# Second norm's scale and shift by TensorE, roots by ScalarE and VectorE, one row by DMA, in a pooling block with a convolutional MLP

## The chip, the cores and the metric

The kernel runs on one core of a Trainium2 chip. Times are microseconds (us) on the device. A core has five engines that run their own instructions in order and wait for each other on semaphores: TensorE (PE, matrix products; PEld is its weight load), VectorE (DVE), ScalarE (ACT), GpSimd (POOL) and SyncE (SP), whose queue issues all of the DMA transfers here.

## What is computed

One layer (DEPTH is 1, so the mixer is the pooling one and the context tokens have no part in the output) on 1024 tokens of width 1024, in float32:

```python
def rms_norm(x, g):
    x32 = x.astype(jnp.float32)
    y = x32 * lax.rsqrt(jnp.mean(x32 * x32, axis=-1, keepdims=True) + EPS)
    return (y * g.astype(jnp.float32)).astype(x.dtype)
...
sh1, sc1, g1, sh2, sc2, g2 = ada_mods(c, ada_w[i], ada_b[i])   # silu(c) @ w + b, six rows of 1024
u = modulate(rms_norm(x, mix_pre_g[i]), sh1, sc1)              # u * (1 + sc1) + sh1
y = pool_mixer(u, pool_w[j], pool_scale[j])                    # four window means, minus u, times four 256x256 matrices
x = x + g1 * rms_norm(y, mix_post_g[i])
f = conv_ffn(modulate(rms_norm(x, ffn_pre_g[i]), sh2, sc2),    # up to 2 x 2816, 3-tap convolution over tokens,
             ffn_w_up[i], ffn_conv_w[i], ffn_conv_b[i], ffn_w_down[i])   # gelu(gate) * val, down to 1024
x = x + g2 * rms_norm(f, ffn_post_g[i])
```

There are four norms over the width: of x, of the mixer's output y, of the sum (the MLP's input), and of the MLP's output. Their mean squares and roots are called x, y, z and o in the kernel.

## The kernel before

Tokens stand on the 128 partitions in eight tiles `x.0` to `x.7`. The program lists its operations with their reads, writes and an estimated time each; a list scheduler at the top of the file then gives them an order for each engine by the longest estimated tail behind an operation, under the room that is left (50 pages of 128x1024 floats, 8 PSUM banks). What it produces is a fixed order for each engine; on the chip each engine goes through its own list and waits where it must. So a changed estimate or a changed operation moves others.

The work runs in these stages.

- **Pooling.** The window means are matrix products with a band matrix that carries the row's root (`band.j`, products `dq`, copies `dt`). For the root, ScalarE squares a tile and sums it along the row (`squares`, into `ms...`), GpSimd adds EPS and raises to the power -0.5 (`rstd`, two instructions, three where the square came in two parts plus one more), and VectorE scales the band.
- **Rows of the condition.** Each of the six rows is silu(c) times a 1024x1024 matrix, loaded in eight pages. `macs` does it on VectorE, one multiply-add pass over 128x1024 for each page, and TensorE sums over the partitions (`cs`, for a row laid out in columns; `g1q`, for a row spread over all partitions). `strips` does it on TensorE: two products of 32 x 512 for each page into one PSUM bank (`st`), a copy by ScalarE (`.acc`) and column sums (`cs`). The MLP's scale and shift come in two halves of 512 columns each, `a2.0.h` (scale) and `a2.1.h` (shift); before, `TUNE["strips"]` names only those of h = 0, and those of h = 1 are sixteen VectorE passes over 128x512.
- **Mixer.** Products `yq.j` with the four matrices, two banks for each token tile, in the order 1, 3, 4, 2, 5, 6, 0, 7. Tiles 0 and 7 need the shift row `sh1` (a VectorE `macs` row) at their edges (`de`). Then, for a tile: squares of yq (two parts), root `ry`, `ty` = yq times the row `grb` (gain times gate), `x` = x + ty * ry, squares of x, root `rz`, `xn` = x * rz. `grb` is a gain row `gr` that TensorE spreads over the partitions (`bcast`, products `rb`) and ScalarE copies, times `g1q`.
- **MLP input.** `xn` of four tiles is transposed (`tq`, first half of the tokens from tiles 1 to 4, second half from 5, 6, 7, 0), scaled and shifted into `u`, and split into a high and a low part (`B11`, `B21` for the first half of the tokens and columns 0 to 511 and 512 to 1023, `B12`, `B22` for the second half), because every product of the MLP is three matrix products of parts (lines L713 to L715).
- **MLP.** Four column blocks (0, 22, 1, 23) are computed plainly in four quarters: `hq`, 64 groups of three products. The other forty go through seven block products in place of eight for two blocks at a time (`X`, `Y`, `Z`), with sums `Bt1` to `Bt4` of the B parts. Then the convolution, gelu, gate, and the down projection in the same manner (`xq`, `zq`, `yb`), with the last norm tile by tile.

Of the kernel before, what the change touches and what calls it, by code (L numbers as in the profile page):

```python
# [195 lines left out]
def pool_ffn_block(ctx, tc, x, c_cols, ada, ada2, ada_bc, ada_br, gains_c, gains_r, pool_w,  # L196
# [359 lines left out]
    macs("g1", NK, first=False)
    for h in range(2):
        op(pe(0.86), lambda e, h=h: e.matmul(t(f"g1q.{h}"), ones, lo_("g1", h), start=True, stop=True), f"g1:{h}",
           f"g1q.{h}")
# [547 lines left out]
```

## Time and profile before

| | |
|---|---|
| three runs | 755.21, 755.69, 756.21 us (median 755.69) |
| profiled execution | 755.83 us, of it 754.1 us span of the engines' instructions |
| TensorE | busy 725.9 us, 96% of the span; mean granted clock 0.979 of full speed |
| VectorE, ScalarE, GpSimd | busy 606.3, 373.7 and 53.0 us |
| from DRAM and to DRAM | 101.91 MB and 19.92 MB |

The profiled execution is 0.14 us above the median. The span is the time from the first instruction to the last; some 1.7 us lie around it. A timeline row gives the start, the duration and, in brackets, how long the engine had stood idle and what released it. TensorE rows count a float32 product as two records, one pass of the weights each.

### The profile page before, as it was taken

The page shows a single profiled execution, that of the slowest core. Times are in us where ns is not written, and L with a number is a line of the kernel's source. Part 1 is how long each engine was busy: PE and PEld are TensorE (multiplying, and loading weights), DVE is VectorE, ACT ScalarE, POOL GpSimd, SP SyncE. Part 2 cuts the span into 40 slices and gives each one's busy share as a digit, 9 for nine tenths or more (in the row PEclk, how much of TensorE's full clock was granted, in tenths as well). Part 3 has the DMA queues.
Part 4 walks back from the last instruction along what each step waited for, and adds up shares of the span by engine and source line. Part 5 has one row for each costly group of instructions (what it writes and reads, how often), then busy time and mean ns, then how long its engine had stood idle before and what let it go on. Part 6 is the DMA issues. An engine that isn't in the chain of part 4 may idle for free.

```text
span 754.1 us, 8995 instructions
## 1 busy us (share of the span) xinstructions
PE 725.9 (96%) x3295; PEld 599.1 (79%) x3295; DVE 606.3 (80%) x759; ACT 373.7 (50%) x546; POOL 53.0 (7%) x73
## 2 busy tenths in 40 slices
PE   7996798999999999999999999999999999999996
PEld 6865686788888888888888888888888888887885
DVE  3986977999877777777777777776879886999974
ACT  6645336865444444444444444444634434337630
POOL 5044014000000000000000000000000000000051
PEclk9997979999999999999999999999999999999998
DMA  8998711013322222222222222206596267998852
GB/s 344 403 399 330 278 56 56 1 56 111 110 83 80 80 80 80 80 79 84 84 83 84 85 84 84 84 28 191 200 356 215 71 193 260 337 380 272 303 194 112
DMA packets 47285, 122.44 MB, mean 162 GB/s; under 512 B 5764, under 2 KB 5892, under 8 KB 47240
## 3 DMA queue, kind: packets, MB, share of 16 engines
q1 hardware_dynamic: 47240, 121.86, 44.9%
q8 instruction: 26, 0.43, 0.2%
q14 instruction: 19, 0.16, 0.1%
HBM read 101.91 MB, written 19.92 MB: 162 GB/s over the span
## 4 chain that ended last, share of the span: by engine, by line
PE 88%; DVE 5%; POOL 2%; DMA 2%; issue 1%; ACT 1%; SPq 0%; DVEq 0%; POOLq 0%; ACTq 0%
PE X L714 10%; PE X L713 10%; PE X L715 10%; PE xq L713 5%; PE xq L715 5%; PE xq L714 5%; PE Z L714 5%; PE Z L715 5%; PE Z L713 5%; PE dq L481 3%; PE zq L713 3%; PE zq L714 3%; PE zq L715 3%; PE Y L714 2%; PE Y L715 2%; PE Y L713 2%
## 5 line engine op out<-in xcount | busy, mean ns | idle before, releaser
L781 ACT ACTIVATE cv<-h,cv 128x1024 f32<-128x1024 f32 x44 | 54.8, 1246 | 104.0 <-DVE h L753 103.2
L783 DVE SCALAR_TENSOR_TENSOR cv<-h,cv,cv 128x1023 f32<-128x1023 f32 x44 | 56.5, 1283 | 24.1 <-ACT cv L781 24.0
L785 DVE SCALAR_TENSOR_TENSOR cv<-h,cv,cv 128x1023 f32<-128x1023 f32 x44 | 56.3, 1279 | 0.8
L747 ACT COPY h<-X 128x512 f32<-128x512 f32 (+1 forms) x80 | 35.8, 474 | 16.4 <-PE X L715 16.4
L753 DVE TENSOR_TENSOR h<-Z,h 128x384 f32<-128x384 f32 (+1 forms) x40 | 15.1, 418 | 33.2 <-PE Z L715 33.2
L879 DVE TENSOR_TENSOR dn<-dn,dn 128x512 f32<-128x512 f32 x55 | 37.2, 685 | 0.0
L970 POOL MEMSET g<- 128x1024 f32 x1 | 1.0, 952 | 496.8 <-PE xq L715 496.8
L753 DVE TENSOR_TENSOR h<-X,h 128x384 f32<-128x384 f32 (+1 forms) x40 | 15.1, 418 | 17.3 <-PE X L715 17.3
L761 DVE TENSOR_TENSOR cv<-cv,cv 128x1024 f32<-128x1024 f32 x22 | 26.8, 1217 | 0.2
L789 ACT ACTIVATE cv<-cv 128x1024 f32<-128x1024 f32 x22 | 23.4, 1063 | 7.0 <-DVE cv L785 4.9
L604 PE MATMUL yq<-wa,dt 128*128 128x256 f32 x96 | 26.4, 435 | 0.0
L604 PEld LDWEIGHTS yq<-wa,dt 128*128 128x128 f32 x96 | 20.9, 222 | 6.0 <-DVE grb L562 0.8
L747 ACT COPY h<-Z 128x384 f32<-128x384 f32 (+1 forms) x40 | 12.9, 376 | 23.7 <-PE Z L715 23.7
L367 ACT ACTIVATE xn<-yq 128x512 f32<-128x512 f32 x16 | 9.5, 597 | 24.0 <-PE yq L604 24.0
L481 PE MATMUL dq<-band,x 128*128 128x136 f32 (+2 forms) x160 | 20.8, 291 | 0.0
L402 DVE SCALAR_TENSOR_TENSOR g<-g,sc,g 128x1024 f32<-128x1024 f32 x14 | 17.9, 1282 | 3.3 <-DMA g<-in_ada 3.2
L481 PEld LDWEIGHTS dq<-band,x 128*128 128x128 f32 x160 | 20.5, 203 | 0.0
L1005 ACT ACTIVATE jk<-ca 128x512 f32<-128x512 f32 (+1 forms) x9 | 5.2, 579 | 23.5 <-DVE ca L1041 23.5
L879 DVE TENSOR_TENSOR dn<-du,dn 128x512 f32<-128x512 f32 x22 | 15.0, 684 | 0.0
L378 POOL TENSOR_SCALAR rso<-mso 128x1 f32<-128x1 f32 x8 | 7.1, 890 | 105.7 <-ACT jk L1005 105.2
L830 DVE TENSOR_TENSOR s<-s,w 128x512 f32<-128x512 f32 x20 | 13.8, 691 | 0.7
L833 DVE TENSOR_TENSOR s<-w,w 128x512 f32<-128x512 f32 x20 | 13.7, 685 | 0.0
(2803 smaller groups left out, 2379.8 us busy)
## 6 DMA issues: line engine op xcount, KB each, us to landing
w<-in_w_up SPq DMA_DIRECT2D x44, 512.0 KB, 5.1
dn<-gd SPq DMA_DIRECT2D x66, 256.0 KB, 4.9
dn<-in_w_down SPq DMA_DIRECT2D x66, 256.0 KB, 5.3
gd<-cv SPq DMA_DIRECT2D x22, 512.0 KB, 3.0
g<-in_ada SPq DMA_DIRECT2D x16, 512.0 KB, 6.7
a<-in_ada SPq DMA_DIRECT2D x16, 512.0 KB, 10.3
du<-in_w_down SPq DMA_DIRECT2D x22, 256.0 KB, 4.3
x<-in_x SPq DMA_DIRECT2D x8, 512.0 KB, 6.0
```

Source lines behind the costliest of these rows:

```text
L481: e.matmul(t(f"dq.{h}.{g}.{cx}")[:, lo - h * H:hi - h * H], t(f"x.{j}")[:, ch:ch + P], bview(j)[:, g, lo - o:hi - o], start=first, stop=la ...
L604: e.matmul(t(f"yq.{j}.{b}")[:, (g % 2) * 256:(g % 2 + 1) * 256], lt, rt, start=(k == 0 and g % 2 == 0), stop=(k == 1), skip_group_check=True)
L713: e.matmul(o, ah[:, s], bh, start=first, stop=False, skip_group_check=True)
L714: e.matmul(o, ah[:, s], bl, start=False, stop=False, skip_group_check=True)
L715: e.matmul(o, al[:, s], bh, start=False, stop=last, skip_group_check=True)
L747: e.copy(t(o)[:, lo:hi], t(b)[:, q:q + hi - lo])
L753: e.tensor_tensor(t(o)[:, lo:hi], t(b)[:, q:q + hi - lo], t(o)[:, lo:hi], ADD)
L761: op(engs or dve(1024), lambda e: e.tensor_tensor(t(o), t(a), t(b), al), f"{a} {b}", o, after=after)
L781: op(act(1024), lambda e: e.activation(t(o), t(h), AF.Identity, bias=cv[:, f, 3:4], scale=cv[:, f, 1:2]), f"{h} cv", o)
L783: op(("V", 1.2), lambda e: e.scalar_tensor_tensor(t(o)[:, 1:T], t(h)[:, 0:T - 1], cv[:, f, 0:1], t(o)[:, 1:T], MUL, ADD), f"{h} cv", o)
L785: op(("V", 1.2), lambda e: e.scalar_tensor_tensor(t(o)[:, 0:T - 1], t(h)[:, 1:T], cv[:, f, 2:3], t(o)[:, 0:T - 1], MUL, ADD), f"{h} cv", o)
L879: op(dve(H), lambda e: e.tensor_tensor(lo_(o, oh), lo_(a, ah), lo_(b, bh), al), f"{a}:{ah} {b}:{bh}", f"{o}:{oh}", after=after)
```

## The change

1. **Roots.** `rstd` leaves GpSimd. ScalarE adds the parts of a mean square (Identity with the other part as bias, once where there are two parts, twice for three) and takes the root (Sqrt with EPS as bias); VectorE takes the reciprocal. This holds for all 32 roots. A first small Sqrt right after the Tanh at the start loads the function table there.
2. **Strips.** `TUNE["strips"]` also names `a2.0.1` and `a2.1.1`, so all four halves of the MLP's scale and shift go through TensorE. The estimate of a pair of strip products falls from 1.1 to 0.45 us. (The code for strips of `sc1` and `g1`, with a table `selb`, is added as well, but the list doesn't name them: those rows and `sh1` stay on VectorE.)
3. **Gain row.** `grb` is loaded by one DMA that reads the row 128 times; the two `rb` products and the two ScalarE copies for it are gone.

```diff
-    "strips": ("a2.0.0", "a2.1.0"),
+    "strips": ("a2.0.0", "a2.1.0", "a2.0.1", "a2.1.1"),
...
+    A.activation(cst("root", [P, 1]), eps, AF.Sqrt)
...
+            elif n == "gr":
+                pg("grb")
+                small_load(lambda: t("grb"), gains_r[1:2].partition_broadcast(P), "grb", 1.4)
...
         def fn(e):
-            ms = stat["m" + key]
-            for k in range(2, n):
-                e.tensor_tensor(ms[:, 1:2], ms[:, 1:2], ms[:, k:k + 1], ADD)
-            e.tensor_scalar(r, ms[:, 0:1], EPS, ms[:, 1:2] if n > 1 else 0.0, ADD, ADD)
-            e.tensor_tensor(r, r, mhalf, ALU.pow)
-        op(("P", 0.7 + 0.2 * n), fn, "", f"m{key} r{key}")
+            for k in range(1, n):
+                e.activation(ms[:, 0:1], ms[:, 0:1], AF.Identity, bias=ms[:, k:k + 1])
+            e.activation(r, ms[:, 0:1], AF.Sqrt, bias=eps)
+        op(("A", 0.25 * n), fn, "", f"m{key} q{key}")
+        op(("V", 0.2), lambda e: e.reciprocal(r, r), f"q{key}", f"r{key}")
...
-            op(pe(1.1), fn, page, b)
+            op(pe(0.45), fn, page, b)
...
-    S.cls = "gr"
-    bcast("gr", 1, "gr", "grb")
```

With other operations and estimates the scheduler gives another order up to the middle of the MLP's first blocks. Three places show it.

On ScalarE, where the roots of tiles 4 and 2 are taken (msz and rsz are mean square and root of the MLP's input, a2_0_0_acc and a2_1_0_acc the copies of the strips for scale and shift of columns 0 to 511), before:

```order
L367 ACTIVATE xn_4_539,msz4_142<-x_4_256 128x1024
L658 CAST pl_22_h__630<-w_22_587 128x1024
L240 ACTIVATE xn_4_539<-x_4_256,rsz4_143 128x1024
L437 COPY a2_0_0_acc_651<-st_a2_0_0_560 128x512
L367 ACTIVATE xn_2_600,msz2_146<-x_2_223 128x1024
L437 COPY a2_1_0_acc_661<-st_a2_1_0_566 128x512
L367 ACTIVATE xn_5_672,msy5_148<-yq_5_0_646 128x512
```
and now:

```order
L454 COPY a2_0_0_acc_583<-st_a2_0_0_561 128x512
L375 ACTIVATE xn_2_596,msy2_152<-yq_2_0_576 128x512
L375 ACTIVATE xn_2_596,msy2_152<-yq_2_1_591 128x512
L386 ACTIVATE msy2_152<-msy2_152 128x1
L387 ACTIVATE rsy2_153<-msy2_152,eps_75 128x1
L375 ACTIVATE xn_1_487,msz1_142<-x_1_216 128x1024
L387 ACTIVATE rsz1_143<-msz1_142,eps_75 128x1
L375 ACTIVATE xn_3_512,msz3_146<-x_3_239 128x1024
L387 ACTIVATE rsz3_147<-msz3_146,eps_75 128x1
L454 COPY a2_1_0_acc_641<-st_a2_1_0_604 128x512
L375 ACTIVATE xn_4_540,msz4_150<-x_4_264 128x1024
L375 ACTIVATE xn_2_596,msz2_154<-x_2_231 128x1024
```
The copies of the strips stood behind the scaling of tile 4, which needs GpSimd's root rsz4. Now the scale's copy stands ahead of all work on tile 2, the shift's copy ahead of the squares of tile 4, and the scaling of tile 4 has gone to VectorE.

On VectorE, around the multiply-add passes of the row sh1 (a2_0_1_acc and a2_1_1_acc are the passes of the MLP's scale and shift for columns 512 to 1023), before:

```order
L402 SCALAR_TENSOR_TENSOR sh1_acc_735<-sh1_2_777,sc_78,sh1_acc_735 128x1024
L644 SCALAR_TENSOR_TENSOR a2_0_1_acc_658<-a2_0_1_2_613,sc_78,a2_0_1_acc_658 128x512 x2
L644 SCALAR_TENSOR_TENSOR a2_1_1_acc_674<-a2_1_1_2_655,sc_78,a2_1_1_acc_674 128x512 x2
L402 SCALAR_TENSOR_TENSOR sh1_acc_735<-sh1_3_803,sc_78,sh1_acc_735 128x1024
L402 SCALAR_TENSOR_TENSOR sh1_acc_735<-sh1_4_813,sc_78,sh1_acc_735 128x1024
L402 SCALAR_TENSOR_TENSOR sh1_acc_735<-sh1_5_824,sc_78,sh1_acc_735 128x1024
L402 SCALAR_TENSOR_TENSOR sh1_acc_735<-sh1_6_833,sc_78,sh1_acc_735 128x1024
L402 SCALAR_TENSOR_TENSOR sh1_acc_735<-sh1_7_844,sc_78,sh1_acc_735 128x1024
L644 SCALAR_TENSOR_TENSOR a2_0_1_acc_658<-a2_0_1_3_623,sc_78,a2_0_1_acc_658 128x512 x2
L644 SCALAR_TENSOR_TENSOR a2_1_1_acc_674<-a2_1_1_3_663,sc_78,a2_1_1_acc_674 128x512 x2
L659 TENSOR_TENSOR pl_23_l__881<-w_23_695,pl_23_h__716 128x1024
```
and now:

```order
L640 SCALAR_TENSOR_TENSOR x_5_270<-ty_5_768,rsy5_157,x_5_270 128x1024
L411 SCALAR_TENSOR_TENSOR sh1_acc_786<-sh1_1_800,sc_79,sh1_acc_786 128x1024
L674 TENSOR_TENSOR a2_1_86<-cs_a2_0_1_818,abc_69 128x4
L676 SCALAR_TENSOR_TENSOR a2_1_86<-a2_1_86,gc_70 128x4
L411 SCALAR_TENSOR_TENSOR sh1_acc_786<-sh1_2_812,sc_79,sh1_acc_786 128x1024
L674 TENSOR_TENSOR sh2_1_88<-cs_a2_1_1_826,abc_69 128x4
L411 SCALAR_TENSOR_TENSOR sh1_acc_786<-sh1_3_824,sc_79,sh1_acc_786 128x1024
L411 SCALAR_TENSOR_TENSOR sh1_acc_786<-sh1_4_835,sc_79,sh1_acc_786 128x1024
L732 TENSOR_TENSOR B21_0_l__873<-u_2_0_846,B21_0_h__861 128x512
L411 SCALAR_TENSOR_TENSOR sh1_acc_786<-sh1_5_849,sc_79,sh1_acc_786 128x1024
L411 SCALAR_TENSOR_TENSOR sh1_acc_786<-sh1_6_864,sc_79,sh1_acc_786 128x1024
L250 TENSOR_SCALAR u_3_0_879<-u_3_0_879,a2_1_86,sh2_1_88 128x512
```
The eight passes of a2 that stood among those of sh1 are gone (eight more stood further up). In their place stand the work of tile 5 and the splits of the B21 parts, which came later before.

On TensorE, from the end of the mixer's tile 6 to the next MLP quarter (cs_sh1 is the column sum of sh1, B21 the second quarter's input), before:

```order
L604 MATMUL yq_6_0_839<-wa_0_447,dt_1_0_372 128x256 x2
L604 MATMUL yq_6_0_839<-wa_0_447,dt_1_1_384 128x256 x2
L416 MATMUL cs_sh1_859<-ones_74,sh1_acc_735 128x1 x8
L416 MATMUL cs_a2_0_1_876<-ones_74,a2_0_1_acc_658 128x1 x4
L416 MATMUL cs_a2_1_1_886<-ones_74,a2_1_1_acc_674 128x1 x4
L713 MATMUL hq_23_0_896<-B11_0_h__728,pl_23_h__716 128x512
```
and now:

```order
L739 MATMUL hq_23_0_857<-B11_1_l__754,pl_23_h__773 128x512
L740 MATMUL hq_23_0_857<-B11_1_h__740,pl_23_l__795 128x512
L629 MATMUL yq_6_0_902<-wa_0_444,dt_1_0_374 128x256 x2
L629 MATMUL yq_6_0_902<-wa_0_444,dt_1_1_395 128x256 x2
L629 MATMUL yq_6_1_916<-wa_1_450,dt_1_2_418 128x256 x2
L629 MATMUL yq_6_1_916<-wa_1_450,dt_1_3_466 128x256 x2
L425 MATMUL cs_sh1_932<-ones_74,sh1_acc_786 128x1 x8
L738 MATMUL hq_0_0_748<-B21_0_h__861,pl_0_h__676 128x512
L739 MATMUL hq_0_0_748<-B21_0_l__873,pl_0_h__676 128x512
```
Before, the MLP's block 23 and half of tile 6 still stood behind the column sum of sh1, with the two column sums of a2 between. Now all four blocks of the first quarter, tile 6 and the column sums of a2 stand ahead of it, and the second quarter follows at once.

## Rows read from the trace of the kernel before

**Rows 1.** The page of the profile: busy time by engine, granted clock in 40 slices, chain.

```profile
PE 725.9 (96%) x3295; PEld 599.1 (79%) x3295; DVE 606.3 (80%) x759; ACT 373.7 (50%) x546; POOL 53.0 (7%) x73
...
PEclk9997979999999999999999999999999999999998
...
PE 88%; DVE 5%; POOL 2%; DMA 2%; issue 1%; ACT 1%; SPq 0%; DVEq 0%; POOLq 0%; ACTq 0%
```

**Rows 2.** Windows, six stages: length, busy time of each engine, clock, DMA share, GB/s.

```profile
28.40:57.90 29.50, 29.50 (x138) 19.84 (x138) 26.60 (x37) 14.43 (x34) 9.71 (x10) 0.94 1.02 402
57.90:90.80 32.90, 21.38 (x101) 18.26 (x100) 26.95 (x34) 15.59 (x27) 7.11 (x9) 0.84 0.84 320
90.80:105.30 14.50, 13.76 (x51) 12.34 (x52) 11.25 (x24) 3.03 (x6) 0.00 (x0) 0.54 0.06 25
105.30:126.40 21.10, 18.00 (x83) 14.99 (x81) 15.38 (x20) 12.16 (x24) 11.78 (x14) 1.00 0.25 101
126.40:154.40 28.00, 27.19 (x131) 21.85 (x132) 27.18 (x30) 23.84 (x35) 0.00 (x0) 1.00 0.04 11
154.40:747.00 592.60, 592.46 (x2641) 490.95 (x2639) 481.32 (x582) 285.02 (x388) 13.48 (x15) 1.00 0.42 146
```

**Rows 3.** Timeline of TensorE: start, duration, what, count, [idle before, what ended it].

```profile
65.42 3.57 PE L446 MATMUL cs_a<-sel,a_acc 128*128 128x1 f32 x16 [7.52 <-ACT a_acc L437]
...
91.28 3.54 PE L416 MATMUL cs_sh<-ones,sh_acc 128*128 128x1 f32 x16 [3.63 <-DVE sh_acc L402]
...
105.76 0.39 PE L713 MATMUL hq<-B_h__912,pl_h__590 128*128 128x512 f32 x1
...
126.39 1.75 PE L682 MATMUL tq<-ident,xn 128*128 128x128 f32 x14 [3.10 <-DVE xn L242]
...
154.06 0.39 PE L713 MATMUL X<-B_h__728,g_h__855 128*128 128x512 f32 x1
```

**Rows 4.** Timeline of ScalarE where a copy stands behind a wait, same columns.

```profile
63.75 1.15 ACT L240 ACTIVATE xn<-x,rsz 128x1024 f32<-128x1024 f32 x1 [5.22 <-POOL rsz L379]
64.81 0.57 ACT L437 COPY a_acc<-st_a 128x512 f32<-128x512 f32 x1
```

**Rows 5.** A group of GpSimd: busy us, mean ns of one, idle before and its releaser.

```profile
L379 POOL TENSOR_TENSOR rsz<-rsz,mhalf 128x1 f32<-128x1 f32 x8 | 10.4, 1300 | 0.7
```

**Rows 6.** Groups of VectorE from 28 to 154 us, same columns.

```profile
L613 DVE TENSOR_TENSOR ty<-yq,grb 128x512 f32<-128x512 f32 x16 | 10.6, 685 | 3.8 <-ACT xn L367 3.6
L644 DVE SCALAR_TENSOR_TENSOR a_acc<-a,sc,a_acc 128x512 f32<-128x512 f32 x14 | 10.2, 749 | 0.3
L615 DVE SCALAR_TENSOR_TENSOR x<-ty,rsy,x 128x1024 f32<-128x1024 f32 x8 | 10.1, 1279 | 0.8 <-POOL rsy L379 0.8
...
L402 DVE SCALAR_TENSOR_TENSOR sh_acc<-sh,sc,sh_acc 128x1024 f32<-128x1024 f32 x7 | 9.0, 1283 | 0.2
L761 DVE TENSOR_TENSOR u<-u,u 128x1024 f32<-128x1024 f32 x6 | 7.3, 1221 | 0.1
```

**Rows 7.** Timelines of ScalarE and VectorE: small operations and the function-table load.

```profile
2.42 0.21 ACT L303 ACTIVATE th<-cc 128x8 f32<-128x8 f32 x1 [0.41 <-DMA cc<-in_c_cols]
4.96 1.06 ACT L367 ACTIVATE band<-x 128x1024 f32<-128x1024 f32 x1 [2.33 <-DMA x<-in_x]
...
156.24 1.28 ACT L789 ACT_TABLE_LOAD   x1
157.54 1.06 ACT L789 ACTIVATE cv<-cv 128x1024 f32<-128x1024 f32 x1
...
2.86 0.17 DVE L305 TENSOR_TENSOR sc<-th,cc 128x8 f32<-128x8 f32 x1
```

**Rows 8.** A group of TensorE from 28 to 154 us: the strips.

```profile
L434 PE MATMUL st_a<-a,scx 128*32 128x512 f32 x32 | 4.7, 598 | 0.0
```

**Rows 9.** Timeline of the end, GpSimd and VectorE.

```profile
747.94 0.43 POOL L377 TENSOR_TENSOR mso<-mso 128x1 f32<-128x1 f32 x1 [5.97 <-ACT jk L1005]
...
749.45 1.42 DVE L1015 SCALAR_TENSOR_TENSOR ca<-ca,rso,x 128x512 f32<-128x512 f32 x2 [1.13 <-POOL rso L379]
```

More of the change, by code (lines that the diff above doesn't have):

```diff
@@ L287, in pool_ffn_block @@
     ident, ones = cst("ident", [P, P]), cst("ones", [P, P])
-    mhalf, scx, sel = cst("mhalf", [P, 1]), cst("scx", [P, NK, 32]), cst("sel", [P, 3])
+    eps, scx, sel = cst("eps", [P, 1]), cst("scx", [P, NK, 32]), cst("sel", [P, 3])
+    selb = cst("selb", [P, 2, P])
     sc, th = cst("sc", [P, NK]), cst("th", [P, NK])
@@ L295, in pool_ffn_block @@
     nc.sync.dma_start(out=cc, in_=c_cols)
-    V.memset(mhalf, -0.5)
+    V.memset(eps, EPS)
+    PL.memset(selb, 0.0)
     V.memset(ones, 1.0)
@@ L301, in pool_ffn_block @@
         V.memset(sel[32 * q:32 * q + 1, 2:3], 1.0)
+        PL.memset(selb[32 * q:32 * q + 1, q % 2], 1.0)
     make_identity(nc, ident)
     A.activation(th, cc, AF.Tanh, scale=0.5)
+    A.activation(cst("root", [P, 1]), eps, AF.Sqrt)
     V.tensor_scalar(th, th, 0.5, 0.5, MUL, ADD)
@@ L319, in pool_ffn_block @@
     pg("g1", "bnd")
-    op(("P", 0.9), lambda e: e.memset(t("g1"), 0.0), "", "g1")
+    if "g1" not in TUNE["strips"]:
+        op(("P", 0.9), lambda e: e.memset(t("g1"), 0.0), "", "g1")
     chunk = {"sc1": 1, "g1": 2, "sh1": 0}
@@ L419, in col_sums, with strips @@
         op(("V", 0.25), lambda e: fin(t(b)[:, 0:n]), f"{b} {deps}", w)
-    def strips(key, pieces):
+    def strips(key, pieces, row=None):
         b = f"st.{key}"
@@ L427, in strips, with fn @@
         seen = set()
+        if row:
+            seen = {0, 1}
+            def fn(e):
+                for q in range(2):
+                    e.matmul(t(b)[32 * q:32 * q + 32, :], ones[0:1, 0:32], t(row)[0:1, q * H:(q + 1) * H], start=True, stop=True,
+                             skip_group_check=True)
+            op(pe(0.45), fn, row, b)
         for page, parts in pieces:
@@ L510, in pool_ffn_block @@
     S.cls = "sc1"
-    macs("sc1", NK)
+    sums = {True: strip_sums, False: col_sums}
+    eight = lambda key: [(f"{key}.{k}", [(lo, k, 2 * (k % 2) + lo) for lo in range(2)]) for k in range(NK)]
+    if "sc1" in TUNE["strips"]:
+        strips("sc1", eight("sc1"))
+    else:
+        macs("sc1", NK)
     S.cls = "psc"
@@ L524, in a1_fin @@
         V.scalar_tensor_tensor(a1, a1, 1.0, gc[:, 0, :], ADD, MUL)
-    col_sums("sc1", NK, a1_fin, "abc gc", "a1")
+    sums["sc1" in TUNE["strips"]]("sc1", NK, a1_fin, "abc gc", "a1")
     S.cls = "wa"
@@ L550, in pool_ffn_block @@
             op(dve(256, 2), fn, f"a1 dt.{e_}.{2 * n} dt.{e_}.{2 * n + 1}", f"de.{e_}:{n}")
-    S.cls = "gr"
-    bcast("gr", 1, "gr", "grb")
     S.cls = "g1"
     bk("g1q.0", "g1q.1")
[L556 to L559, printed above, removed]
+    if "g1" in TUNE["strips"]:
+        strips("g1", eight("g1"), row="g1")
+        for h in range(2):
+            op(pe(0.86), lambda e, h=h: e.matmul(t(f"g1q.{h}"), selb[:, h], lo_("g1.acc", 0), start=True, stop=True), "g1.acc",
+               f"g1q.{h}")
+    else:
+        macs("g1", NK, first=False)
+        for h in range(2):
+            op(pe(0.86), lambda e, h=h: e.matmul(t(f"g1q.{h}"), ones, lo_("g1", h), start=True, stop=True), f"g1:{h}",
+               f"g1q.{h}")
     S.cls = "g1q"
@@ L566, in pool_ffn_block @@
     if "sh1" in TUNE["strips"]:
-        strips("sh1", [(f"sh1.{k}", [(lo, k, 2 * (k % 2) + lo) for lo in range(2)]) for k in range(NK)])
+        strips("sh1", eight("sh1"))
     else:
         macs("sh1", NK)
-    sums = {True: strip_sums, False: col_sums}
     S.cls = "sh1f"
```

1 line of the change is left out of this document (added).

## The prediction

> **What bounds the kernel now.** I read the page first. TensorE is busy for 96% of the span and the chain of what ended last runs through it for 88%; the granted clock, slice by slice, is below full only in the first six of 40 slices, apart from the last [rows 1]. So the question is where TensorE is not busy or not at full clock. The table by stage answers it: from 154.4 to 747 it is busy 592.46 of 592.60 us at full clock, and nothing can be won there but by less work. From 57.9 to 154.4 it stands for 16.2 us (11.52, 0.74, 3.10 and 0.81 of the four windows), and in two of these windows the mean clock is 0.84 and 0.54 [rows 2]. Half clock (1.2 of 2.4 GHz) shows as 0.5, so it ruled for about (1 - 0.84) x 2 x 32.9 = 10.5 us and (1 - 0.54) x 2 x 14.5 = 13.3 us.
>
> Then TensorE's timeline, to see what ended those gaps. There are three large ones: 7.52 us until 65.42 for ScalarE's copy of the strips, 3.63 us until 91.28 for VectorE's last pass of sh1, 3.10 us until 126.39 for the last xn [rows 3]. Behind the first, on ScalarE, the copy stood in line after the scaling of tile 4, which had waited 5.22 us for GpSimd's root [rows 4]. GpSimd's power takes 1.30 us on average for 128 numbers [rows 5], and each root is two such instructions, behind each other. The windows name VectorE as the next busiest: 26.95 of 32.9 us from 57.9 to 90.8.
>
> **The change part by part.** *Roots.* The nearest rows for a ScalarE instruction on 128x1 and a VectorE one are 0.21 us (128x8) and 0.17 us (128x8) [rows 7]. A root is then 0.21 + 0.17 us, with a sum of two parts 0.59, and some 0.1 us for each hand-over; on GpSimd it took above 1.3. Bounds for the ScalarE part: not below the 0.17 of the VectorE row, and at worst the 0.57 us of the copy of 128x512 [rows 4], which would add 0.36 to each instruction: some nine of them stand on the path below (roots of tiles 4, 2 and 7, the last norm), 3.2 us, 741.6 for the sum. I take 0.21, whose shape is nearest. In place of GpSimd's separate queue the roots now stand in ScalarE's, where they delay the squares behind them; ScalarE is busy 15.59 of 32.9 us in the densest stage of the mixer, so 13 roots there (some 5 us) fit.
>
> *Table loads.* Sqrt needs a function table of its own; the new order holds four loads, two more than before: behind the Tanh, and at the first root of the last norm. A load took 1.28 us, and the next instruction began 1.30 after it had begun [rows 7]. The early one lies between the Tanh's end at 2.63 and the first square at 4.96: with a 0.21 us root it ends at 4.14, hidden by the load of x, and costs 1.3 if that came sooner. The late one lies under the last products of TensorE, which is busy there; I put both at nothing. The Trainium skill (ScalarE: Activation LUTs, What ACT_TABLE_LOAD costs) puts a switch at about 2.66 us, because a drain of about 1.38 follows the load. The row above shows no such drain; by the page's figure the early load would end about 0.5 us after x has landed, an estimate, and the sum below would be 738.9 in place of 738.4.
>
> *Gain row.* The products and copies of gr leave; a transfer of 0.52 MB joins a queue that moves 402 GB/s in that stage, all it can (DMA share 1.02) [rows 2]: 0.52 / 402 is 1.3 us later for all loads behind. The next step, the gate's product, waits for VectorE's passes over g1, which the change leaves as they are, so I count nothing either way; if that cover went, 1.3 us, 739.7.
>
> *Strips.* Sixteen VectorE passes go: fourteen at 0.749 us and two starters, at most the same each [rows 6]. TensorE gets as many strip products as it has now, 4.7 us [rows 8], in place of nothing (the column sums stay).
>
> *Where the time then goes.* I work through the three gaps with the new order. First VectorE, up to the last pass of sh1, on which tiles 0 and 7 depend. From 57.9 to 90.8 it was busy 26.95 us. Twelve of the sixteen passes lay there, at most 9.0 us. What now stands ahead of the last sh1 pass and did not: the work of tile 5 (two passes of 0.685, one of 1.279), three B21 splits (0.685 each), the split of block 23 (1.22), and some thirteen reciprocals and small instructions at 0.17, 2.2, together 8.1 [rows 6, 7]. So VectorE is about as busy as before: 26.95 - 9.0 + 8.1 = 26.1 us. Its idle time there was 5.95; the waits for GpSimd and for the late column sums go, others come for ScalarE's roots, and I keep 4.0, with 2.0 as the lower bound (two waits of a hand-over and a root for each of the tiles 4, 2 and 5). Starting 0.5 us early, as the two row products ahead are gone, the last sh1 pass ends at 57.4 + 26.1 + 4.0 = 87.5, and the gap's end moves from 91.28 to 87.7: **3.6 us**.
>
> Second, what TensorE still had to do after that gap: 14.48 us from 91.28 to the first product with B21 at 105.76 [rows 3], most of it at half clock. Of this only the column sum of sh1 remains, 3.54 us at half clock, 1.8 at full. **12.7 us** go. The rest (block 23, half of tile 6, column sums of a2) must fit into the earlier stretch. There TensorE was busy 21.38 of 32.9 us; 3.6 of that was half clock (cs_a and what followed it for 7.2 us); added are about 2.8 for block 23, 1.9 for half a tile, 1.8 for column sums, 4.7 for strips: 21.4 - 3.6 + 11.2 = 29.0, against 87.7 - 57.4 = 30.3. It fits with 1.3 us to spare.
>
> Third, the gap of 3.10 before 126.39. GpSimd's roots for tiles 0 and 7 are gone, and the order now puts two product groups behind the transposes, but tile 7's chain (squares, root, x, squares, root, xn) still runs across three engines. I take the gap as closed, less 0.5 us for the wait of tile 0's edge, which moves up behind sh1: **2.6 us**.
>
> Fourth, the tail: from GpSimd's first sum at 747.94 to the multiplication at 749.45 [rows 9] are 1.51 us; now three ScalarE instructions and a reciprocal, 3 x 0.21 + 0.17 + 0.2 = 1.0. **0.5 us**.
>
> The sum is 3.6 + 12.7 + 2.6 + 0.5 = 19.4. I take off 2 us for hand-overs that these steps don't count (some twenty, 0.1 each): 17.4. The profiled execution took 755.83 us, 0.14 above the median; 755.83 - 17.4 = **738.4 us**. The first X product, at 154.06 [rows 3], would start at about 137.
>
> **The rivals.** *The clock falls again.* For it: both low stretches lie about a long gap, and the shortened stretch is nearly full, so a wait in it could bring one. Against: the waits named above go. One fall of the shorter old length, 10.5 us, costs up to 5.2, of which the 1.3 to spare covers some: 4 us, 742.4.
>
> *The strips' copies and the roots stay late on ScalarE's queue.* They wait there behind squares that wait for VectorE, as the old copy waited behind a scaling. Then the first gap stays half as long, 3.8 us, with a low clock after it, and the third stays whole: 17.4 - 3.8 - 3.6 - 2.6 = 7.4 won, 748.4. For it: both queues run in order, and the order puts the shift's copy behind two squares of z. Against: no instruction in front of it waits for more than one VectorE pass.
>
> *No faster.* TensorE's clock falls again and again up to X. Half clock for L us loses L / 2 of work, so the gain of 17.4 is gone at L = 34.8 us. From 57.9 to 105.3 it ruled for 23.8, about long gaps; both old lengths and the longer one once more make 37.1 us, a loss of 18.6: 757.0. Against it: from 105.3 on the clock was full in spite of the 3.10 gap [rows 2]. The Trainium skill (TensorE: Matmul & The Clock Gate, HAM oscillation) says that an engine with gaps can go on swinging between the two clocks; the windows at 0.84 and 0.54 agree that it falls, the ones after don't show it lasting.
>
> **How the numbers follow.** 62 in 100 for 738.4 (its own range 734.4 to 741.6), 20 for 742.4, 12 for 748.4, 6 for a result not below 754, of which 4 for slower. From the bounds: without the allowance 736.4, and with VectorE's waits at 2.0 us 734.4; at the other end the rivals up to 748.4. So the range is 734.4 to 748.5. About 0.2% is what a measurement can tell here. Faster has 0.94, the same 0.02, slower 0.04.
>
> **What would show it.** In the new profile: no GpSimd work between 2 and 500 us; the column sum of sh1 on TensorE near 88, with all sixteen groups of the first quarter ahead of it; the wait ahead of the first column sum of the strips under 1 us; clock at or near full from 50 to 137; X at about 137; the last multiplication 1.0 us after the last square's sum. The prediction is wrong if VectorE idles more than 6 us between 57 and 88, if the clock row is below 9 anywhere from slice 5 to 30, or if the stage from X on is longer than 592.6, because splits that were pushed behind X are then late.

## The result and the profile after

The changed kernel takes 735.70 us (median of four runs, 735.27 to 736.65); the kernel before took 755.45 us beside it (753.26 to 756.21). The ratio is 0.9745, with a 95% interval of 0.9722 to 0.9768: 19.7 us faster, where 17.4 were forecast. The profiled execution took 735.27 us. One execution of e7, an experiment below, took 913 us at a mean granted clock of 0.751 and is left out.

From the page of the changed kernel: the span, the busy time of each engine, the granted clock in 40 slices, and the chain of what ended last.

```profile
span 733.5 us, 9033 instructions
PE 717.0 (98%) x3323; PEld 589.1 (80%) x3323; DVE 600.5 (82%) x778; ACT 386.8 (53%) x595; POOL 3.7 (0%) x13
PEclk9999999999999999999999999999999999999998
PE 89%; DVE 4%; DMA 3%; ACT 2%; issue 1%; SPq 0%; DVEq 0%; ACTq 0%
```

The low slices of [rows 1] are gone, and GpSimd, 53.0 us before, has 3.7. The windows by stage (us, then busy time and instructions of each engine, granted clock, DMA share, GB/s):

```profile
28.40:57.40 29.00, 27.87 (x160) 20.94 (x160) 28.43 (x46) 15.33 (x41) 0.00 (x0) 1.00 1.03 409
57.40:88.00 30.60, 29.92 (x171) 21.53 (x171) 27.97 (x44) 21.87 (x41) 0.00 (x0) 1.00 1.01 389
88.00:106.00 18.00, 16.64 (x76) 13.63 (x76) 16.74 (x30) 12.28 (x30) 0.00 (x0) 1.00 0.24 98
106.00:134.00 28.00, 27.54 (x136) 22.34 (x135) 19.18 (x23) 20.57 (x31) 0.00 (x0) 1.00 0.00 1
134.00:726.00 592.00, 592.00 (x2637) 490.57 (x2636) 488.55 (x594) 293.18 (x407) 0.95 (x1) 1.00 0.42 146
```

In the stretch in which TensorE was busy 21.38 of 32.9 us at a clock of 0.84 [rows 2], it is now busy 29.92 of 30.6 at full clock. TensorE's timeline (start, duration; in brackets the idle time ahead and what ended it) shows what became of the three gaps of [rows 3]:

```profile
53.45 1.05 PE L463 MATMUL cs_a<-sel,a_acc 128*128 128x1 f32 x8
56.47 1.05 PE L463 MATMUL cs_a<-sel,a_acc 128*128 128x1 f32 x8
62.20 1.97 PE L707 MATMUL tq<-ident,xn 128*128 128x128 f32 x16
...
86.03 1.92 PE L425 MATMUL cs_sh<-ones,sh_acc 128*128 128x1 f32 x16 [0.68 <-DVE sh_acc L411]
87.81 0.48 PE L738 MATMUL hq<-B_h__861,pl_h__676 128*128 128x512 f32 x1
...
105.73 0.85 PE L707 MATMUL tq<-ident,xn 128*128 128x128 f32 x6 [1.23 <-ACT h L772]
...
133.98 0.39 PE L738 MATMUL X<-B_h__721,g_h__923 128*128 128x512 f32 x1
```

The column sums of the strips (`cs_a`, 7.52 us of idle ahead of them before) start without a wait. Ahead of `cs_sh` stand 0.68 us in place of 3.63, and behind it comes the first product with B21 (87.81) at once. The wait for the last xn, 3.10 us before, is gone; ahead of the transposes at 105.73 TensorE now waits 1.23 us for ScalarE's copies of `h`, which the forecast did not count. The marks of the two timelines add up to the whole difference:

| stretch of TensorE's timeline | before | after | won | forecast |
|---|---|---|---|---|
| up to the column sum of sh1 | 91.28 | 86.03 | 5.25 | 3.6 |
| from there to the first product with B21 | 14.48 | 1.78 | 12.70 | 12.7 |
| from there to the first X product | 48.30 | 46.17 | 2.13 | 2.6 |
| from there to the end of the span | 600.04 | 599.52 | 0.52 | 0.5 |
| sum | | | 20.60 | 19.4, less an allowance of 2.0 |

The spans differ by just that, 754.1 - 733.5 = 20.6.

### The profile page after: what moved, and what is told of

It is laid out like the page before. It is cut to its first block, busy times and chain, and to the rows that moved or that the text cites. A ratio compares the mean times of both kernels' runs of the same rounds, so it can differ in the third digit from the quotient of the medians.

```text
span 733.5 us, 9033 instructions
## 1 busy us (share of the span) xinstructions
PE 717.0 (98%) x3323; PEld 589.1 (80%) x3323; DVE 600.5 (82%) x778; ACT 386.8 (53%) x595; POOL 3.7 (0%) x13
## 4 chain that ended last, share of the span: by engine, by line
PE 89%; DVE 4%; DMA 3%; ACT 2%; issue 1%; SPq 0%; DVEq 0%; ACTq 0%
PE X L738 10%; PE X L740 10%; PE X L739 10%; PE xq L739 5%; PE xq L740 5%; PE xq L738 5%; PE Z L740 5%; PE Z L739 5%; PE Z L738 5%; PE zq L739 3%; PE zq L738 3%; PE zq L740 3%; PE Y L740 2%; PE Y L739 2%; PE Y L738 2%; PE yq L629 2%
## 5 line engine op out<-in xcount | busy, mean ns | idle before, releaser
L772 ACT COPY h<-Z 128x384 f32<-128x384 f32 (+1 forms) x40 | 12.9, 377 | 23.1 <-PE Z L740 21.3
L629 PE MATMUL yq<-wa,dt 128*128 128x256 f32 x96 | 21.8, 382 | 0.0
L629 PEld LDWEIGHTS yq<-wa,dt 128*128 128x128 f32 x96 | 18.0, 190 | 4.0 <-DVE rsz L389 0.8
L498 PE MATMUL dq<-band,x 128*128 128x136 f32 (+2 forms) x160 | 20.6, 290 | 0.0
L854 DVE TENSOR_TENSOR s<-w 128x512 f32<-128x512 f32 x20 | 13.7, 684 | 0.0
L860 DVE TENSOR_TENSOR s<-w,s 128x512 f32<-128x512 f32 x20 | 13.7, 684 | 0.0
```

The costliest lines, as they stand in the source:

```text
L498: e.matmul(t(f"dq.{h}.{g}.{cx}")[:, lo - h * H:hi - h * H], t(f"x.{j}")[:, ch:ch + P], bview(j)[:, g, lo - o:hi - o], start=first, stop=la ...
L629: e.matmul(t(f"yq.{j}.{b}")[:, (g % 2) * 256:(g % 2 + 1) * 256], lt, rt, start=(k == 0 and g % 2 == 0), stop=(k == 1), skip_group_check=True)
L772: e.copy(t(o)[:, lo:hi], t(b)[:, q:q + hi - lo])
```

## Experiments

The forecast gave the first gap to GpSimd's roots and the second to the sixteen VectorE passes. So the parts were taken apart. Each row is a kernel; "price" is the scheduler's estimate of a pair of strip products, and each ratio is to the kernel before, run beside it.

| kernel | roots | second half of scale/shift | gain row | price | us | ratio, 95% |
|---|---|---|---|---|---|---|
| before | GpSimd | VectorE | TensorE | 1.1 | 755.4 to 756.4 | 1 |
| e3_row_only | GpSimd | VectorE | DMA | 1.1 | 753.58 | 0.9961 to 0.9985 |
| e9_price_only | GpSimd | VectorE | TensorE | 0.45 | 753.81 | 0.9953 to 0.9986 |
| e1_roots_only | ScalarE | VectorE | TensorE | 1.1 | 750.03 | 0.9918 to 0.9958 |
| e10_second_half_on_dve | ScalarE | VectorE | DMA | 0.45 | 748.46 | 0.9868 to 0.9905 |
| e8_price | ScalarE | strips | DMA | 1.1 | 744.91 | 0.9823 to 0.9885 |
| e4_no_row | ScalarE | strips | TensorE | 0.45 | 741.97 | 0.9807 to 0.9856 |
| e2_strips_only | GpSimd | strips | TensorE | 0.45 | 741.79 | 0.9784 to 0.9877 |
| e5_no_roots | GpSimd | strips | DMA | 0.45 | 738.58 | 0.9725 to 0.9784 |
| changed | ScalarE | strips | DMA | 0.45 | 735.70 | 0.9722 to 0.9768 |

The kernel before had a median of 755.42 us beside e1 to e4, 756.42 beside e5 to e8 and 755.99 beside e9 to e12, so differences of medians across these groups are uncertain by up to about 2 us. The kernels e6, e7, e11 and e12 follow in the text.

### One part at a time, and the gain row taken back

Against the kernel before, e1 has the lines of the change on `rstd` and the early Sqrt only, and e3 those on `gr` and `grb` only (e1, e2 and e3 also hold the change's unused code for strips of `sc1` and `g1`). The edit of e2 is

```diff
-    "strips": ("a2.0.0", "a2.1.0"),
+    "strips": ("a2.0.0", "a2.1.0", "a2.0.1", "a2.1.1"),
...
-            op(pe(1.1), fn, page, b)
+            op(pe(0.45), fn, page, b)
```

and e4 is the changed kernel with the transfer taken back:

```diff
-            elif n == "gr":
-                pg("grb")
-                small_load(lambda: t("grb"), gains_r[1:2].partition_broadcast(P), "grb", 1.4)
...
+    S.cls = "gr"
+    bcast("gr", 1, "gr", "grb")
```

> The kernel before with the roots alone moved to ScalarE and VectorE (early Sqrt included); strips, gain row and the planner's price of a strip as before. My theory: the 19 us have two halves. Roots on GpSimd make the 7.52 us gap at 57.9 and its low clock; the sixteen VectorE passes over the second half of the scale and shift make the last pass of sh1 late and leave work behind it. With the roots alone the first half is won: no gap above 2 us at the first column sum of the strips, but VectorE has some 44 us of work up to the last sh1 pass (39 in the changed kernel, by the counts of its order and the durations of its rows), so that pass ends near 91 in place of 86 and TensorE, which has 8 us less to do ahead of it, stands 8 to 13 us there. Time 746 (743 to 750). Rival A, the waits for GpSimd were all of it: 738 or less, at most 2 us above the changed kernel. Rival B, the roots alone win nothing since VectorE sets the end: 753 to 756.

> The kernel before with all four accumulations in strips (and the strip priced at 0.45) alone; roots on GpSimd, gain row by TensorE. My theory: VectorE's work up to the last sh1 pass falls to some 35.5 us (38.3 before), but the waits for GpSimd's roots stay, so that pass ends near 88.5; the order leaves only 6 products of the first quarter behind it. The first gap stays at 4 to 7 us with a low clock about it, and the gap for the last xn stays at 3. Time 743 (739 to 748), GpSimd busy 7 us or more between 57 and 88, granted clock in a slice there below 9 tenths. Rival A (waits for GpSimd are all): 752 to 756. Rival C, the VectorE passes were all of it: 736 to 738.

> The kernel before with the gain row by a broadcast transfer alone. Removes two TensorE products and two ScalarE copies and adds a 0.52 MB transfer; roots and strips as before. My theory: nothing is won by itself, and the other order that comes out of the planner puts more VectorE work (43 us against 38) ahead of the last sh1 pass: 755, between 751 and 760. Rival: the transfer delays the loads behind it by 1.3 us and all of that is seen: 757.

> The changed kernel with the gain row made by TensorE and ScalarE again: roots and strips as changed. My theory: the row is worth nothing, the time is that of the changed kernel, 735.7, within 1.5 us. Rival: the transfer costs 1.3 us of load time on the path: 734.4. Other rival: two products and two copies more at the place where TensorE is full cost 0.9 us or more: 736.6 to 738.

Measured: 750.03, 741.79, 753.58 and 741.97 us. Against the runs beside them the roots alone win 5.4 us, the strips 13.6, the transfer 1.8. In TensorE's timeline with the roots alone, two gaps stay:

```profile
63.27 3.02 PE L460 MATMUL cs_a<-sel,a_acc 128*128 128x1 f32 x16 [2.63 <-ACT a_acc L451]
89.83 3.54 PE L422 MATMUL cs_a<-ones,a_acc 128*128 128x1 f32 x16 [6.09 <-DVE a_acc L668]
```

The first shrank from 7.52 to 2.63 us, not quite to the 2 of the expectation, and the second, 6.09 us, is now for VectorE's passes; the time is just above the stated 743 to 750. Rival A, the waits for GpSimd as the whole cause, is out. With the strips alone (and their price), roots still on GpSimd, the largest gap from 28 us to the first X product is 1.38 us (TensorE's timeline of e2):

```profile
65.39 1.86 PE L705 MATMUL tq<-ident,xn 128*128 128x128 f32 x15 [1.38 <-DVE xn L242]
```

There the expectation was wrong, which had 4 to 7 us ahead of the first column sums and 3 more at the last xn. So the first gap closes, but for this rest, without touching the roots.

The kernel e4 is the other surprise: without the transfer the time is 6.3 us longer, where the forecast had counted nothing. Its first X product starts at 137.96, 3.98 us later than in the changed kernel. One part is the two products themselves (TensorE's timeline of e4):

```profile
45.11 1.98 PE L392 MATMUL rb_gr<-gr,ones 1*128 1x512 f32 x4
```

In the changed kernel TensorE has an idle 0.87 us at that place, so they cost about 1.1. The rest lies in two stretches of low clock (0.57 from 32 to 36 us, which costs 1.7 us, and 0.86 and 0.71 from 84 to 92, another 1.7), and behind X in a wait of 1.1 us for a copy of h that the changed kernel doesn't have. That the other order is the cause of all this is not shown: e6 below has the changed kernel's order and a clock of 0.65 from 32 to 36 us as well.

### The engine of the roots, with the order held

The kernel e5 is the changed kernel with `rstd` as it was before, so that the order is made anew. In e6 the entries of the list stay as changed, and with them the order on TensorE, ScalarE, VectorE and SyncE, but what they issue for a root goes to GpSimd (the early Sqrt leaves too):

```diff
-            for k in range(1, n):
-                e.activation(ms[:, 0:1], ms[:, 0:1], AF.Identity, bias=ms[:, k:k + 1])
-            e.activation(r, ms[:, 0:1], AF.Sqrt, bias=eps)
+            if n > 1:
+                PL.tensor_scalar(r, ms[:, 0:1], EPS, ms[:, 1:2], ADD, ADD)
+            else:
+                PL.tensor_scalar(r, ms[:, 0:1], EPS, 0.0, ADD, ADD)
+            for k in range(2, n):
+                PL.tensor_tensor(r, r, ms[:, k:k + 1], ADD)
+            PL.tensor_tensor(r, r, mhalf, ALU.pow)
         op(("A", 0.25 * n), fn, "", f"m{key} q{key}")
-        op(("V", 0.2), lambda e: e.reciprocal(r, r), f"q{key}", f"r{key}")
+        op(("V", 0.2), lambda e: None, f"q{key}", f"r{key}")
```

> The changed kernel with its roots on GpSimd again (strips and gain row as changed; the planner puts the order anew). The runs so far: roots alone won 5.4 us, strips alone 13.6, strips and roots without the gain row 13.5, so roots on top of strips gave nothing. My theory of the prediction, in which GpSimd's roots make the first gap and its low clock: 741 to 747. Rival, which those runs speak for: with the second half of the sums in strips the transposes of tiles 1 to 4 have other TensorE work ahead of them, and GpSimd's roots are hidden; what is left of them is the tail, 0.5 us, and small waits: 735 to 738.

> The changed kernel in its own order on TensorE, ScalarE, VectorE and SyncE, but each root is carried out by GpSimd at the place where ScalarE and VectorE had it (the Sqrt, the Identity sums and the reciprocal leave). It asks what the engine of the root is worth when the order is not made for it. If the time of a root counts, the scaling of each tile waits some 2 us more and the order has no other work there: 740 to 748, with idle time of TensorE ahead of the transposes. If the order covers it: 736 to 738.

Measured: e5 738.58 us, whose interval overlaps that of the changed kernel, and e6 736.02 us (0.9698 to 0.9758), which can't be told from it. The forecast's reading of the roots falls with this: in the changed kernel's order it makes no difference that a run can tell whether ScalarE and VectorE or GpSimd take them. In e6 the scaling of each tile does wait for GpSimd, in small pieces (VectorE's, GpSimd's and TensorE's timelines):

```profile
53.62 3.67 DVE L644 SCALAR_TENSOR_TENSOR x<-ty,rsy,x 128x1024 f32<-128x1024 f32 x3
...
58.67 0.75 DVE L242 TENSOR_SCALAR xn<-x,rsz 128x1024 f32<-128x1024 f32 x1 [0.72 <-POOL rsz L391]
60.19 0.75 DVE L242 TENSOR_SCALAR xn<-x,rsz 128x1024 f32<-128x1024 f32 x1 [0.50 <-POOL rsz L391]
61.70 0.75 DVE L242 TENSOR_SCALAR xn<-x,rsz 128x1024 f32<-128x1024 f32 x1 [0.76 <-POOL rsz L391]
...
55.07 1.45 POOL L391 TENSOR_TENSOR rsz<-rsz,mhalf 128x1 f32<-128x1 f32 x1
...
58.72 0.79 POOL L388 TENSOR_SCALAR rsz<-msz 128x1 f32<-128x1 f32 x1
59.59 0.56 POOL L391 TENSOR_TENSOR rsz<-rsz,mhalf 128x1 f32<-128x1 f32 x1
60.24 0.79 POOL L388 TENSOR_SCALAR rsz<-msz 128x1 f32<-128x1 f32 x1
...
62.40 1.98 PE L711 MATMUL tq<-ident,xn 128*128 128x128 f32 x16
```

The last of the four is scaled by 62.45, and TensorE turns to the transposes at 62.40 without a wait, since strips of the second half (1.91 us from 57.65, 1.05 from 61.41) and products of the mixer between them stand ahead. This work covers the roots. (In e6 the sums of the last norm stand in another order, so that its tail has one GpSimd instruction less than before.)

### The order alone

The kernel e8 is the changed kernel with the old price; e9 is the kernel before with the new one, the same line the other way round.

```diff
-            op(pe(0.45), fn, page, b)
+            op(pe(1.1), fn, page, b)
```

> The changed kernel with the planner's price of a strip at 1.1 as before, in place of 0.45: the same instructions in another order. By the counts, VectorE has 33 us of work up to the last sh1 pass in place of 39, and all the products of tiles 5 to 7 stand behind the column sum of sh1 instead of partly ahead. If only the sum of TensorE's work counts, 735 to 737. If the order counts as well as the operations, as the kernel without the gain row's transfer suggests (two products take 2 us, it lost 6.3): 738 to 743, with low clock in the first 110 us or gaps above 1 us.

> The kernel before, with the planner's price of a strip at 0.45 in place of 1.1 and nothing else: the same instructions in another order. With the price of 1.1 the changed kernel lost 9 us and had the first gap back (4.14 us for the strips' copies, which stood behind eight squares and roots on ScalarE), although its roots were on ScalarE and VectorE. Theory: the first gap belongs to the order, so it closes here too, with the roots still on GpSimd; the second (sixteen VectorE passes, last sh1 pass near 91) and the gap for tile 7's xn stay: 748 (744 to 751), first gap under 2 us. Rival, the roots make the first gap: 753 to 757, gap of 5 us or more ahead of the first column sum of the strips or the first transposes.

Measured: 744.91 us, above the 738 to 743 expected, and 753.81 us. In e8 every root is on ScalarE and VectorE, and a first gap is there all the same, 4.14 us. The rows are of its ScalarE and of its TensorE (the profiled execution, 747.98 us, is the longest of four):

```profile
59.15 1.04 ACT L375 ACTIVATE xn<-x 128x1024 f32<-128x1024 f32 x1
60.09 0.18 ACT L375 ACTIVATION_READ_ACCUMULATOR xn<-x 128x1 f32 x1
60.19 0.46 ACT L387 ACTIVATE rsz<-msz,eps 128x1 f32<-128x1 f32 x2
60.56 1.04 ACT L454 COPY a_acc<-st_a 128x512 f32<-128x512 f32 x2
...
61.17 3.57 PE L463 MATMUL cs_a<-sel,a_acc 128*128 128x1 f32 x16 [4.14 <-ACT a_acc L454]
```

At the old price the copies of the strips stand behind the squares and roots of four tiles, and TensorE waits for them; the clock is 0.88 and 0.83 in the two windows up to 88 us. This is the rival of the late copies, in an order that the change didn't make. So the time does not depend on the operations alone: one estimate is worth 9.2 us by the medians, and 8.2 by the ratios, (0.9854 - 0.9745) x 755.45. The strips' gain hangs on it too: at the old price, strips and gain row add 5.1 us to the roots (e8 against e1). In e9, with the new price but neither strips nor new roots, the copies come early and the gap moves to the next thing, the scaled tiles; the second gap grows (TensorE's timeline, then GpSimd's):

```profile
66.64 3.80 PE L682 MATMUL tq<-ident,xn 128*128 128x128 f32 x19 [3.33 <-DVE xn L242]
90.88 3.54 PE L416 MATMUL cs_sh<-ones,sh_acc 128*128 128x1 f32 x16 [9.00 <-DVE sh_acc L402]
...
64.34 1.45 POOL L379 TENSOR_TENSOR rsz<-rsz,mhalf 128x1 f32<-128x1 f32 x1
```

Here nothing covers GpSimd's roots (the last one ends at 65.79), so both theories had half of it: the place of the copies and the roots can each make a gap up to the transposes. The expected 748 was too low by 6 us, because VectorE's passes took the place at once: the 9.00 us.

### The second half on VectorE, and sh1 in strips too

Both are the changed kernel with another list of strips, the first line below in e10, the second in e11.

```diff
-    "strips": ("a2.0.0", "a2.1.0", "a2.0.1", "a2.1.1"),
+    "strips": ("a2.0.0", "a2.1.0"),
...
+    "strips": ("a2.0.0", "a2.1.0", "a2.0.1", "a2.1.1", "sh1"),
```

> The changed kernel with the second half of the scale and shift on VectorE again (only the table's two entries leave; roots, gain row and the price of 0.45 stay). VectorE has 43 us of work up to the last sh1 pass by the counts, against 39: that pass ends near 90 in place of 85.9. Theory: this is the second half of what was won, and no order hides it: a gap of 4 us or more ahead of the column sums near 88 with a low clock behind it, 745 (742 to 750), the first gap under 2 us. Rival, the price and the order are all of it: 736 to 738.

> The changed kernel with the shift of the first norm (sh1) in strips as well: eight VectorE passes of 1.28 us leave, 16 more strip products of 0.24 us each come to TensorE, 3.8 us. If VectorE's passes still set the end, it wins: 731 to 735. If TensorE's own work does, which the changed kernel's windows say (3.7 us of idle time in all from 28.5 to the first X product, 1.1 of it for sh1), it loses 3.8 less the 1.1 and something for its other waits: 738 (736.5 to 740).

Measured: 748.46 and 748.16 us. In e10 all but the sixteen passes is as changed, in an order made anew, and the loss is 12.8 us by the medians (10.7 by the ratios), which TensorE's timeline places where the theory has it:

```profile
79.79 1.02 PE L425 MATMUL cs_a<-ones,a_acc 128*128 128x1 f32 x8 [2.54 <-DVE a_acc L669]
89.04 1.83 PE L425 MATMUL cs_a<-ones,a_acc 128*128 128x1 f32 x8 [8.23 <-DVE a_acc L669]
```

In e11 TensorE has no gap above 0.5 us from 30 us to X, as expected, but the loss is 12.5 us (10.7 by the ratios) instead of 2 or 3. The price of the strips was wrong. Its group, and single rows of the timeline:

```profile
L451 PE MATMUL st_sh<-sh,scx 128*32 128x512 f32 x32 | 8.4, 605 | 0.0
...
31.16 4.93 PE L498 MATMUL dq<-band,x 128*128 128x8 f32 x20
78.84 1.05 PE L451 MATMUL st_sh<-sh,scx 128*32 128x512 f32 x4
```

Each pair of strip products stands alone here, between products of the MLP, column sums and transposes, and takes 1.05 us; the sixteen strips cost 8.4 us, not 3.8. Two pairs behind each other take hardly longer than one, as a row of TensorE's timeline in e9 shows (x8 records are two pairs):

```profile
54.62 1.07 PE L434 MATMUL st_a<-a,scx 128*32 128x512 f32 x8
```

Besides, 20 small products of e11 took 4.93 us with the clock at 0.50 from 32 to 36 us, 2.60 in the changed kernel, and behind X one wait took 2.2 us. Together 8.4 + 2.3 + 2.2 = 12.9, less the closed wait of 0.68 at sh1: near the 12.4 by which the spans differ.

### TensorE's work where it waits, and where it doesn't

In e7 each of the two row products of g1 is made twice, in the changed kernel's order:

```diff
-            op(pe(0.86), lambda e, h=h: e.matmul(t(f"g1q.{h}"), ones, lo_("g1", h), start=True, stop=True), f"g1:{h}",
-               f"g1q.{h}")
+            op(pe(0.86), lambda e, h=h: [e.matmul(t(f"g1q.{h}"), ones, lo_("g1", h), start=True, stop=True)
+                                         for _ in range(2)], f"g1:{h}", f"g1q.{h}")
```

In e12 the pool's scale comes by a transfer as well, queued behind sc1 (its place in the list of loads is changed too):

```diff
-            elif n == "gr":
-                pg("grb")
-                small_load(lambda: t("grb"), gains_r[1:2].partition_broadcast(P), "grb", 1.4)
+            elif n in ("gr", "psr"):
+                pg(f"{n}b")
+                small_load(lambda n=n, i=i: t(f"{n}b"), gains_r[i:i + 1].partition_broadcast(P), f"{n}b", 1.4)
...
-    bcast("psr", 1, "psr", "psrb")
```

> The changed kernel, in its own order, with each of the two row products of g1 made twice: 1.98 us more of TensorE work at the place where the kernel without the gain row's transfer has its two products of the gain row (rb_gr 1.98 us, at 45.11). Leaving out the transfer cost 6.3 us in all. If TensorE's own time is what the gain row saves, this costs 2.0 us: 737.7 (737.2 to 738.2). If such products stand beside a wait for VectorE that is there anyway, as I had counted: 735.7 to 736.2. The rest of the 6.3 us is then the other order and the clock.

> The changed kernel with the other broadcast row, the pool's scale, brought by a transfer too (queued behind the loads of sc1): two products of TensorE at 5.35 to 9.1 leave (3.75 us) and two ScalarE copies, and a transfer of 0.52 MB stands ahead of the pool's weights. If TensorE's work counts wherever it is, up to 3 us are won: 732 to 734. If it counts only where TensorE is the engine waited for, nothing is won here, since the first column sum at 28.5 waits for VectorE's passes over sc1, which follow their loads: 735.7, within 1.5, with a longer gap ahead of that column sum.

Measured: e7 738.58 us as the median of five runs from 737.87 to 742.89, e12 736.45 us with a ratio of 0.9717 to 0.9753. In e7's profile X starts at 136.61, 2.63 us later. The doubled products take 3.60 us in place of 1.96, and the idle 0.87 ahead of them is gone: 0.8 net. The 20 small `dq` products in front ran at a low clock in this execution (0.71 from 32 to 36 us; they took 4.26 us, 2.60 in the changed kernel), which is the larger part. So e7 is no clean measure of the 2.0 us; that the clock fell there because of the edit is not shown, as the edit lies behind it. In e12 the first column sum starts 0.73 us earlier than in the changed kernel, 27.80 in place of 28.53, behind VectorE's last pass over sc1, and the 3.75 us that TensorE no longer spends ahead of it bring no gain. The gap ahead of that sum is 0.43 us, 1.01 in the changed kernel, so it did not grow as expected: TensorE waits until 7.21 us for another load and then needs 19.49 us for the products that took 18.01. And the clock is 0.94 from 28.4 to 57.4 us in e12, so it is no clean measure either.

## Why the prediction was right, and where its reasons were not

**What was to be seen.** GpSimd does nothing in the windows from 28.4 to 134 us, the clock is full in them, all sixteen groups of the first quarter stand ahead of the column sum of sh1, and the strips' column sums don't wait. That sum stands at 86.03 for "near 88", X at 133.98 for 137.

**Size.** The sum of the four terms was 19.4, and the four stretches of the timeline won 20.6. The allowance of 2.0 for hand-overs was the mis-sized step: from 57.4 to 88 us TensorE idles 30.6 - 29.92 = 0.68 us in all, and that is the one wait ahead of the column sum of sh1. The first term was too small by 1.65, in VectorE's idle time: its busy time from 57.4 to the end of the last sh1 pass is 25.87 us (26.1 forecast), but the pass ends at 85.89, not 87.5:

```profile
84.61 1.28 DVE L411 SCALAR_TENSOR_TENSOR sh_acc<-sh,sc,sh_acc 128x1024 f32<-128x1024 f32 x1
```

So VectorE idled 28.5 - 25.87 = 2.6 us, where 4.0 were kept and 2.0 was the bound.

**The strips (12.7, the largest term).** Right in size and, by e10, in cause: with the passes back on VectorE a gap of 8.23 us opens, and 12.8 us are lost. That this loss is so near the term of 12.7 says little: it is spread over the whole way to X, which starts 13.15 us later than in the changed kernel. On TensorE the strips of all four halves take 9.8 us, about twice the 4.7 of [rows 8]:

```profile
L451 PE MATMUL st_a<-a,scx 128*32 128x512 f32 x64 | 9.8, 600 | 0.0
```

**The roots.** Here the step failed that read the first gap as GpSimd's: "waited 5.22 us for GpSimd's root" was true of the kernel before [rows 4], but its going was not what the change needed. That the sum held in spite of it is luck: the change also held what closes this gap without the roots. Taken alone the roots win 5.4 us; on top of strips and gain row, in the same order, nothing that a run can tell (e6). Strips ahead of the transposes cover them, and the price that puts the copies early closes the gap at the copies (e8 has fast roots and keeps 4.14 us of it). The two remedies overlap, so their gains don't add: 5.4 and 13.6 alone, 13.5 together without the row. Nor was GpSimd's root two instructions of 1.30 us: the sum ahead of the power took 0.48 us on average for rsz before (first row below). The costs of the new root were 0.29 us on ScalarE, under the bound but above the 0.21 taken, and 0.15 on VectorE, where 0.17 was taken (the other rows, of the changed kernel):

```profile
L378 POOL TENSOR_SCALAR rsz<-msz 128x1 f32<-128x1 f32 x8 | 3.8, 477 | 17.8 <-ACT xn L367 17.6
...
L387 ACT ACTIVATE rsz<-msz,eps 128x1 f32<-128x1 f32 x8 | 2.2, 291 | 0.2
...
L389 DVE RECIPROCAL rsy<-rsy 128x1 f32<-128x1 f32 x8 | 1.2, 154 | 0.0
```

**The table loads.** Nothing, as forecast. ScalarE's timeline:

```profile
2.65 1.28 ACT L307 ACT_TABLE_LOAD   x1
3.95 0.20 ACT L307 ACTIVATE root<-eps 128x1 f32<-128x1 f32 x1
4.67 1.06 ACT L375 ACTIVATE band<-x 128x1024 f32<-128x1024 f32 x1 [0.51 <-DMA x<-in_x]
...
703.00 1.28 ACT L387 ACT_TABLE_LOAD   x1
704.30 0.29 ACT L387 ACTIVATE rso<-mso,eps 128x1 f32<-128x1 f32 x1
```

The next instruction begins 1.30 us after a load has begun, twice. The Trainium skill (ScalarE: Activation LUTs, What ACT_TABLE_LOAD costs) counts a drain of about 1.38 us more; no run here shows it, and the first square still waits for x.

**The gain row.** Counted at nothing because the gate's product waits for VectorE. It does, for 0.87 us, as rows of VectorE and TensorE in the changed kernel show:

```profile
43.29 1.41 DVE L416 SCALAR_TENSOR_TENSOR g<-g,sc,g 128x512 f32<-128x512 f32 x2
...
44.14 1.96 PE L584 MATMUL g1q<-g,ones 128*128 128x512 f32 x4 [0.87 <-PE yq L629]
```

The first of the two passes ends near 44.0, and the product begins 0.1 us behind it, though the bracket names TensorE itself. So some 1.1 of the two products' 1.98 us counted: the step that put the row at nothing failed by that much. The other 5 us of e4 are not the products' own time, and what part of them the order makes is not shown; alone the row won 1.8.

**The tail.** From the first sum to the multiplication it is 1.16 us now and 1.51 before [rows 9]: 0.35 won, not 0.5, since an instruction on ScalarE takes 0.29 us and not 0.21:

```profile
727.76 0.60 ACT L386 ACTIVATE mso<-mso 128x1 f32<-128x1 f32 x2
728.40 0.29 ACT L387 ACTIVATE rso<-mso,eps 128x1 f32<-128x1 f32 x1
728.72 0.16 DVE L389 RECIPROCAL rso<-rso 128x1 f32<-128x1 f32 x1 [0.41 <-ACT rso L387]
728.92 1.42 DVE L1040 SCALAR_TENSOR_TENSOR ca<-ca,rso,x 128x512 f32<-128x512 f32 x2
```

The other 0.17 of the table's 0.52 lie elsewhere behind X, so that this term came out is in part luck.

**The rivals.** None came true here: the clock is full from 28 to 134 us, and no copy is late. Both are real, though: e8 is the late copies, with 744.9 us for the 748.4 worked out, and e1, e8, e9 and e10 show a low clock about and behind their gaps (window means of 0.63 to 0.89 from 57.4 to 106 us; in e8 the clock is full again from 88).

## What to carry to other kernels

When a scheduler makes the order, a trace of the new kernel does not say which edit won: hold the order and swap the operation (e6), then hold the operations and swap the order (e8). A wait can be closed by making what is waited for shorter or by other work that stands ahead of it; whoever does both is paid once. Work given to the bound engine should be priced as it will stand, alone or behind its like (e11). That work taken off it counts only where it isn't waiting anyway is argued from the traces of e4 and e12; no run here prices it cleanly.
